# A layer norm without affine: one in-place ring of 48 rows a partition, tiles of 16 rows tapering to 8, 4, 2, 2

## Chip, cores, metric

One core of one Trainium2 chip. The metric is the device time of one execution in microseconds (us); several executions of each kernel were timed. A run also has a profile with the span from its first to its last instruction; the metric stands about 2 us above the span. "Fast" and "slow" are states of a run: one over 1.5% above the fastest of its kernel is called slow and left out of ratios.

## The reference

Every row of 1024 float32 numbers is brought to mean 0 and variance 1. There are 32 x 512 = 16384 rows, 67.1 MB in and 67.1 MB out.

```python
mean = np.mean(x, axis=-1, keepdims=True)
var = np.var(x, axis=-1, keepdims=True)
return ((x - mean) / np.sqrt(var + eps)).astype(np.float32)
```

## The kernel before

A tile takes 4 rows on each of 128 partitions (16 KiB of contiguous memory a partition, 2 MiB in all), so there are 32 tiles. Input and output have six buffers each. VectorE (DVE) makes the statistics, ScalarE (ACT) the square root and the normalisation, GpSimd (POOL) one small product. Loads are issued by SyncE (SP), stores by ACT.

```python
K = 4
...
xin = ctx.enter_context(tc.tile_pool(name="xin", bufs=6))
yout = ctx.enter_context(tc.tile_pool(name="yout", bufs=6))
...
for t in range(ntiles):
    xt = xin.tile([P, K, D], fdt)
    nc.sync.dma_start(out=xt, in_=x2[rows].rearrange("(p k) d -> p k d", p=P))
    # bn_stats on two halves of each row and bn_aggr: mv = mean, variance
    ...
    nc.vector.tensor_scalar_mul(out=negmean, in0=mv[:, :, 0], scalar1=-1.0)
    nc.vector.tensor_scalar(out=vpe, in0=mv[:, :, 1], scalar1=eps_val, ...)
    nc.vector.reciprocal(out=ivar, in_=vpe)
    nc.scalar.activation(out=rstd, in_=ivar, func=AF.Sqrt, ...)
    nc.gpsimd.tensor_mul(out=nmr, in0=negmean, in1=rstd)
    yt = yout.tile([P, K, D], fdt)
    for k in range(K):
        nc.scalar.activation(out=yt[:, k, :], in_=xt[:, k, :], func=AF.Identity,
                             bias=nmr[:, k : k + 1], scale=rstd[:, k : k + 1])
    nc.scalar.dma_start(out=dst, in_=yt)
```

The order of the source is not the order in which an engine issues its instructions. A scheduler lays that order down when the kernel is built.

## Time and profile before

| | |
|---|---|
| time | 321.08 us (320.97 to 321.26, 3 runs) |
| span of the profiled run | 319.0 us |
| busy | DVE 57%, ACT 48%, POOL 2% |
| rate while the stream is full | 431 GB/s |

The page's DMA row gives in tenths how busy the core's 16 DMA engines are in each of 40 slices of the span. An order-of-time line has start, duration, engine, source line, operation, output<-input, count, and in brackets the idle time before it with what ended it. A line of waits has the total in us, how often, and the longest.

### The profile page before, as it was taken

The numbers are of one execution on the slowest core, as the hardware profiler recorded it, in microseconds if no ns is written. First come the engines' busy times: TensorE is split into PE (matmuls) and PEld (weight loads), VectorE is DVE, ScalarE is ACT, GpSimd is POOL, SyncE is SP. The second block draws the span as 40 slices with busy tenths as digits, with TensorE's granted clock in tenths as the row PEclk, the third lists the DMA queues.
The fourth block names the chain that finished last, engine by engine and source line by source line (L and its number), as shares of the span: only waits on it lengthen the run. The fifth ranks groups of instructions, "written<-read, shape, count | busy, mean of one in ns | idle before, by whom it ended". The sixth has DMA issues, their size and how long they took to land.

```text
span 319.0 us, 926 instructions
## 1 busy us (share of the span) xinstructions
DVE 181.6 (57%) x480; ACT 154.3 (48%) x161; POOL 6.6 (2%) x36
## 2 busy tenths in 40 slices
DVE  0999764457754477544676355765446744467610
ACT  1147491651907419074380833809247091470970
POOL 0000000000000000000000000000000000000000
DMA  7999999999999999999999999999999999999995
GB/s 294 427 405 422 438 431 431 431 429 431 426 429 432 435 431 431 429 427 431 431 433 435 430 431 427 427 431 427 435 438 430 428 431 427 431 427 427 421 427 220
DMA packets 9222, 134.27 MB, mean 421 GB/s; under 512 B 1024, under 2 KB 1024, under 8 KB 1024
## 3 DMA queue, kind: packets, MB, share of 16 engines
q1 hardware_dynamic: 4608, 67.11, 49.6%
q10 hardware_dynamic: 4608, 67.11, 49.2%
q14 instruction: 6, 0.05, 0.0%
HBM read 67.11 MB, written 67.11 MB: 421 GB/s over the span
## 4 chain that ended last, share of the span: by engine, by line
DMA 87%; DVE 4%; issue 3%; ACT 2%; SPq 1%; POOLq 0%; POOL 0%; DVEq 0%
DMA xt<-in_x_dram 87%; DVE stats L53 3%; ACT yt L75 1%; SPq L47 1%; DVE mv L57 0%; DVE ivar L65 0%; DVE negmean L59 0%; POOLq L115 0%; ACT rstd L68 0%; POOL nmr L71 0%; DVE vpe L61 0%; DVEq L65 0%; DVEq L59 0%
## 5 line engine op out<-in xcount | busy, mean ns | idle before, releaser
L53 DVE BATCH_NORM_STATS2 stats<-xt 128x6 f32<-128x512 f32 x256 | 159.4, 665 | 115.3 <-DMA xt<-in_x_dram 115.3
L75 ACT ACTIVATE yt<-xt,nmr,rstd 128x1024 f32<-128x1024 f32 x128 | 146.7, 1227 | 4.7 <-POOL nmr L71 4.5
L68 ACT ACTIVATE rstd<-ivar 128x4 f32<-128x4 f32 x32 | 6.6, 205 | 149.6 <-DVE ivar L65 149.0
L57 DVE BATCH_NORM_AGGREGATE mv<-stats 128x2 f32<-128x12 f32 x128 | 25.1, 196 | 1.1
L71 POOL TENSOR_TENSOR nmr<-negmean,rstd 128x4 f32<-128x4 f32 x32 | 6.3, 198 | 297.9 <-ACT rstd L68 297.9
L65 DVE RECIPROCAL ivar<-vpe 128x4 f32<-128x4 f32 x32 | 5.7, 178 | 3.0
L59 DVE TENSOR_SCALAR negmean<-mv 128x4 f32<-128x4 f32 x32 | 5.4, 170 | 3.1
L61 DVE TENSOR_SCALAR vpe<-mv 128x4 f32<-128x4 f32 x32 | 5.2, 162 | 0.0
L68 ACT ACT_TABLE_LOAD x1 | 1.3, 1283 | 0.7 <-PEq L101 0.7
L101 POOL MEMSET const-float32-0.0<- 128x1 f32 x1 | 0.1, 98 | 0.2 <-issue 0.2
L101 POOL MEMSET const-uint8-127<- 128x1 uint8 x1 | 0.1, 102 | 0.0
L101 POOL MEMSET const-bfloat16-1.0<- 128x1 bf16 x1 | 0.1, 101 | 0.0
L101 POOL MEMSET const-float32-1.0<- 128x1 f32 x1 | 0.1, 98 | 0.0
## 6 DMA issues: line engine op xcount, KB each, us to landing
xt<-in_x_dram SPq DMA_DIRECT2D x32, 2048.0 KB, 38.4
out_dram<-yt ACTq DMA_DIRECT2D x32, 2048.0 KB, 15.5
```

What stands on the lines that cost most here:

```text
L47: nc.sync.dma_start(out=xt, in_=x2[rows].rearrange("(p k) d -> p k d", p=P))
L53: nc.vector.bn_stats(out=stats[:, k, s, :], in_=xt[:, k, s * BN_MAX : (s + 1) * BN_MAX],)
L57: nc.vector.bn_aggr(out=mv[:, k, :], in_=stats[:, k, :, :])
L59: nc.vector.tensor_scalar_mul(out=negmean, in0=mv[:, :, 0], scalar1=-1.0)
L61: nc.vector.tensor_scalar(out=vpe, in0=mv[:, :, 1], scalar1=eps_val, scalar2=None, op0=ALU.add)
L65: nc.vector.reciprocal(out=ivar, in_=vpe)
L68: nc.scalar.activation(out=rstd, in_=ivar, func=AF.Sqrt, bias=0.0, scale=1.0)
L71: nc.gpsimd.tensor_mul(out=nmr, in0=negmean, in1=rstd)
L75: nc.scalar.activation(out=yt[:, k, :], in_=xt[:, k, :], func=AF.Identity, bias=nmr[:, k : k + 1], scale=rstd[:, k : k + 1],)
L101: nc = _bacc.Bacc("TRN2", target_bir_lowering=False, num_devices=1)
```

## The change

The intent: fewer and larger DMAs with runs of 64 KiB (a DMA run is one contiguous piece of one partition, and one record in the DMA trace), no second set of buffers, and small last tiles so that the final store is short. The same 192 KiB of each partition now form one ring of 48 rows, in which a tile is loaded, normalised in place and stored. Statistics go by groups of 8 rows. The small operations are reordered: the square root is taken of the variance plus eps on ACT, then DVE takes the reciprocal and one fused product; POOL does nothing.

```diff
+TILES = (16, 16, 16, 16, 16, 16, 16, 8, 4, 2, 2)
+RING = 48
+GROUP = 8
...
-    xin = ctx.enter_context(tc.tile_pool(name="xin", bufs=6))
-    yout = ctx.enter_context(tc.tile_pool(name="yout", bufs=6))
+    ring = ring_pool.tile([P, RING, D], fdt)
...
+    for K in TILES:
+        if pos + K > RING:
+            pos = 0
+        xt = ring[:, pos : pos + K, :]
         nc.sync.dma_start(out=xt, in_=x2[rows].rearrange("(p k) d -> p k d", p=P))
+        for g in range(0, K, GROUP):
+            # bn_stats, bn_aggr for G rows
...
+            nc.scalar.activation(out=std[:, :G], in_=mv[:, :G, 1], func=AF.Sqrt, bias=eps_t, scale=1.0)
+            nc.vector.reciprocal(out=rstd[:, :G], in_=std[:, :G])
+            nc.vector.scalar_tensor_tensor(out=nmr[:, :G], in0=mv[:, :G, 0], scalar=-1.0,
+                                           in1=rstd[:, :G], op0=ALU.mult, op1=ALU.mult)
+            for k in range(G):
+                nc.scalar.activation(out=xt[:, g + k, :], in_=xt[:, g + k, :], func=AF.Identity, ...)
-        nc.scalar.dma_start(out=dst, in_=yt)
+        nc.scalar.dma_start(out=o2[rows].rearrange("(p k) d -> p k d", p=P), in_=xt)
```

More of the change, by code (lines that the diff above doesn't have):

```diff
@@ L26 @@
     BN_MAX = nc.vector.BN_STATS_FMAX
-    assert D % BN_MAX == 0
     NSUB = D // BN_MAX
-    K = 4
-    rows_per_tile = P * K
-    assert N % rows_per_tile == 0
-    ntiles = N // rows_per_tile
-    xin = ctx.enter_context(tc.tile_pool(name="xin", bufs=6))
-    yout = ctx.enter_context(tc.tile_pool(name="yout", bufs=6))
+    assert sum(TILES) * P == N
+    ring_pool = ctx.enter_context(tc.tile_pool(name="ring", bufs=1))
     st = ctx.enter_context(tc.tile_pool(name="st", bufs=4))
+    const = ctx.enter_context(tc.tile_pool(name="const", bufs=1))
     fdt = mybir.dt.float32
@@ L41 @@
     ALU = mybir.AluOpType
-    for t in range(ntiles):
-        rows = slice(t * rows_per_tile, (t + 1) * rows_per_tile)
-        xt = xin.tile([P, K, D], fdt)
-        nc.sync.dma_start(out=xt, in_=x2[rows].rearrange("(p k) d -> p k d", p=P))
-        stats = st.tile([P, K, NSUB, 6], fdt)
-        mv = st.tile([P, K, 2], fdt)
-        for k in range(K):
-            for s in range(NSUB):
-                nc.vector.bn_stats(
-                    out=stats[:, k, s, :],
-                    in_=xt[:, k, s * BN_MAX : (s + 1) * BN_MAX],
-                )
-            nc.vector.bn_aggr(out=mv[:, k, :], in_=stats[:, k, :, :])
-        negmean = st.tile([P, K], fdt)
-        nc.vector.tensor_scalar_mul(out=negmean, in0=mv[:, :, 0], scalar1=-1.0)
-        vpe = st.tile([P, K], fdt)
-        nc.vector.tensor_scalar(
-            out=vpe, in0=mv[:, :, 1], scalar1=eps_val, scalar2=None, op0=ALU.add
-        )
-        ivar = st.tile([P, K], fdt)
-        nc.vector.reciprocal(out=ivar, in_=vpe)
-        rstd = st.tile([P, K], fdt)
-        nc.scalar.activation(out=rstd, in_=ivar, func=AF.Sqrt, bias=0.0, scale=1.0)
-        nmr = st.tile([P, K], fdt)
-        nc.gpsimd.tensor_mul(out=nmr, in0=negmean, in1=rstd)
-        yt = yout.tile([P, K, D], fdt)
-        for k in range(K):
-            nc.scalar.activation(
-                out=yt[:, k, :],
-                in_=xt[:, k, :],
-                func=AF.Identity,
-                bias=nmr[:, k : k + 1],
-                scale=rstd[:, k : k + 1],
-            )
-        dst = o2[rows].rearrange("(p k) d -> p k d", p=P)
-        nc.scalar.dma_start(out=dst, in_=yt)
@@ new lines @@
+    ring = ring_pool.tile([P, RING, D], fdt)
+    eps_t = const.tile([P, 1], fdt)
+    nc.vector.memset(eps_t, eps_val)
+    row = 0
+    pos = 0
+    for K in TILES:
+        if pos + K > RING:
+            pos = 0
+        xt = ring[:, pos : pos + K, :]
+        rows = slice(row * P, (row + K) * P)
+        nc.sync.dma_start(out=xt, in_=x2[rows].rearrange("(p k) d -> p k d", p=P))
+        for g in range(0, K, GROUP):
+            G = min(GROUP, K - g)
+            stats = st.tile([P, GROUP, NSUB, 6], fdt, name="stats")
+            mv = st.tile([P, GROUP, 2], fdt, name="mv")
+            for k in range(G):
+                for s in range(NSUB):
+                    nc.vector.bn_stats(
+                        out=stats[:, k, s, :],
+                        in_=xt[:, g + k, s * BN_MAX : (s + 1) * BN_MAX],
+                    )
+                nc.vector.bn_aggr(out=mv[:, k, :], in_=stats[:, k, :, :])
+            std = st.tile([P, GROUP], fdt, name="std")
+            nc.scalar.activation(
+                out=std[:, :G], in_=mv[:, :G, 1], func=AF.Sqrt, bias=eps_t, scale=1.0
+            )
+            rstd = st.tile([P, GROUP], fdt, name="rstd")
+            nc.vector.reciprocal(out=rstd[:, :G], in_=std[:, :G])
+            nmr = st.tile([P, GROUP], fdt, name="nmr")
+            nc.vector.scalar_tensor_tensor(
+                out=nmr[:, :G],
+                in0=mv[:, :G, 0],
+                scalar=-1.0,
+                in1=rstd[:, :G],
+                op0=ALU.mult,
+                op1=ALU.mult,
+            )
+            for k in range(G):
+                nc.scalar.activation(
+                    out=xt[:, g + k, :],
+                    in_=xt[:, g + k, :],
+                    func=AF.Identity,
+                    bias=nmr[:, k : k + 1],
+                    scale=rstd[:, k : k + 1],
+                )
+        nc.scalar.dma_start(out=o2[rows].rearrange("(p k) d -> p k d", p=P), in_=xt)
+        row += K
+        pos += K
```

## The prediction

> **What bounds the kernel now.** I read the page first (parts 1, 2, 4 and 6), then the busy time by stretch, then the waits and the order of time on the engines.
>
> ```profile
> DVE 181.6 (57%) x480; ACT 154.3 (48%) x161; POOL 6.6 (2%) x36
> ...
> DMA  7999999999999999999999999999999999999995
> ...
> HBM read 67.11 MB, written 67.11 MB: 421 GB/s over the span
> ...
> DMA 87%; DVE 4%; issue 3%; ACT 2%; SPq 1%; POOLq 0%; POOL 0%; DVEq 0%
> ...
> out_dram<-yt ACTq DMA_DIRECT2D x32, 2048.0 KB, 15.5
> ```
>
> No compute engine is near full, and the DMA row is full from the second slice to the last but one. The busy time by stretch gives the rate of the full stream and its two ends:
>
> ```profile
> core 0: us, DVE busy (x) ACT busy (x) POOL busy (x), PEclk, DMA share, GB/s
> ...
> 60.00:200.00 140.00, 79.60 (x210) 69.26 (x73) 2.78 (x14) 1.00 1.01 431
> ...
> 314.00:316.00 2.00, 0.00 (x0) 0.00 (x0) 0.00 (x0) 1.00 0.66 279
> ...
> 317.00:318.00 1.00, 0.00 (x0) 0.00 (x0) 0.00 (x0) 1.00 0.04 16
> ```
>
> The stream runs at 431 GB/s. 134.27 MB at that rate take 311.5 us; the span is 319.0, so ramp and drain together cost only 7.5 us. A change here can win little unless the stream itself gets faster, but it can lose much if the stream runs dry. What could make it run dry shows in the order of time on ACT between 19 and 32 us:
>
> ```profile
> 19.61 0.38 ACTq L84 DMA_DIRECT2D out_dram<-yt  x1
> 20.11 0.21 ACT L68 ACTIVATE rstd<-ivar 128x4 f32<-128x4 f32 x1 [0.53 <-DVE ivar L65]
> 25.78 0.20 ACT L68 ACTIVATE rstd<-ivar 128x4 f32<-128x4 f32 x1 [5.47 <-DVE ivar L65]
> 25.89 5.75 ACT L75 ACTIVATE yt<-xt,nmr,rstd 128x1024 f32<-128x1024 f32 x5
> ```
>
> Tile 1's square root is done at 20.3, yet its four normalisations start only at 25.89: the scheduler has put tile 2's square root ahead of them, so ACT sits 5.47 us waiting for the statistics of a later tile. The list of waits says how common this is:
>
> ```profile
> ACT rstd L68 <- DVE ivar L65: 149.0, 19, 12.4
> ```
>
> With six input and six output buffers of 2 MiB this read-ahead costs nothing: the queues hold enough work while ACT waits.
>
> **What the Trainium skill says.**
> 1. DMA: Bandwidth & Descriptors, section "Where 436 GB/s comes from": a fabric ceiling of 435 GB/s. The trace agrees: 431. So larger runs can win at most about 1%, 311.5 to 308.7 us (estimate from that page's ceiling).
> 2. The same page, "Anatomy of one DMA": DMA engines do not wait on semaphores; the issuing sequencer does. So a load held back by a buffer, and a store held back by ACT, are absent from the queues. This kernel's trace agrees in the list of the DMA queue's own waits, where SP waits before it issues a load.
> 3. PSUM — Partial Sum Buffer, "Engine vs sequencer instructions": "ScalarE/VectorE/GpSimdE queues are strict FIFO." The 5.47 us above agree: work that was ready did not pass the square root ahead of it.
> 4. Perfetto Trace Analysis, "Optimization Strategy": consistent bubbles on the engine that should be saturated can mean too few buffers for the next tile. The DMA row before shows none; I expect the changed kernel to show them.
>
> **The change part by part.**
> Small work: 32 each of negmean (170 ns), vpe (162), reciprocal (178) go, 16.3 us of DVE; 18 groups with a reciprocal and one fused operation at about 180 ns come back, 6.5. DVE falls to about 172 us, ACT from 154.3 to about 151, POOL to nothing. All beside DMA: 0 us on the path.
> Descriptors: 64 KiB runs for 16 KiB and 22 DMAs for 64. Stream gain 0 to 3 us, see 1.
> Buffers: 12 x 16 KiB = 192 KiB a partition before, and 48 x 4 KiB = 192 KiB now; the bytes are equal but the grain is 3 slots of 8 MiB. Load k+3 waits for the whole store k. One big tile takes 8.39 MB / 431 = 19.5 us alone, 39 when a load and a store share.
> Order: I compared the instruction order of the two builds. In the new ACT stream the square root of tile 2's second group is followed by those of both groups of tile 3, and only then come tile 2's last eight normalisations. The same holds for tile 4 against both groups of tile 5. Store 2 therefore waits for load 3 and its statistics, store 4 for load 5. At the end, the square roots of the 8-, 4- and first 2-row tile precede the second half of tile 6; on DVE that half's reciprocal also follows the first statistics of the last tile. Also tile 6's first half comes behind three statistics instructions of the 8-row tile. So store 6, 8 MiB, waits until the very last load has landed: the taper is defeated.
>
> Worked timetable, from measured pieces: statistics 1.26 us a row (10.40 to 11.66 in the order of time, i.e. two halves and an aggregate), 20.2 a tile; normalisation 4.63/4 = 1.15 a row, 9.2 a group; 2.2 us per hand-off from a finished store to the next load's data (my choice: the first load is issued at 0.73 and used at 8.60, 3.0 us more than its 4.87 at 431, part of it ramp).
> - Loads 0, 1, 2 stream from 2. Load 0 lands at 22; group 0 is normalised at 36-45, group 1 at 46-55; store 0 is issued at 55, load 2 shares with it and lands at 65.
> - Store 0 ends at 80; load 3 needs it and nothing else is queued: idle 2.2.
> - Tile 1's second reciprocals sit behind tile 2's first statistics, so store 1 comes only at 93. Load 3 lands at 110, store 1 ends at 121.5: idle 2.2 again, load 4 from 124.
> - Statistics of tile 3 end at 130; tile 2's second half runs to 140; store 2 at 141. Load 4 lands at 145; store 3 at 159 and load 5 from 165 share to about 200.
> - Load 6 runs alone from 202 to 221.5. Store 4 waits for statistics of tile 5 (203-223), then ACT 224-233, issue 234, data 235.6: idle 14.
> - Store 4 alone to 255; then the last four loads (waiting for store 4) beside store 5. All that, 37 us of work, ends at 294.
> - The last load lands at 295; last statistics, then tile 6's second half 299-308; store 6 at 309.6, data 311: idle 16.6.
> - Stores 6 to 10 are 32 rows = 16.8 MB = 39 us: last byte at 350.
> Idle sum: 2.2 + 2.2 + 14.1 + 16.6 = 35. Span: 350 + 1.1 for the end (before: last packets in 317-318, span 319.0) = 351. The metric stood 2.1 above the span before (321.08 to 319.0): 353. Slow DMA engines: every idle is set by the slowest of 16, whose drift before was hidden by queued work; the drain from 314 to 318 shows some 2 us. For several exposed joints I add 2, and take 1 off for larger runs: **354 us**, +10%.
>
> **Rivals.**
> A. Stream stays full. If every tile were normalised when ready, a store would follow its landing by about 31 us (20.2 + 9.2 + small) within a 39 us period, and DMA would never idle: 308.7 to 311.5 plus 7.5, so 317 to 320 in span, 319 to 322 in the metric. For it: DVE 57%, ACT 48%. Against it: the order above is static, and 5.47 us show that ACT obeys it.
> B. Gain by larger runs plus the short last store: 314 to 318. Needs A and a faster stream; the ceiling leaves 1%, and the small last store can't help when store 6 waits for the last load.
> C. Unequal sharing. If the DMA engines alternate by descriptor, the 8-, 4- and 2-row loads (32, 16, 8 KiB runs) get a smaller share beside store 5 (64 KiB) and land later in the order; the same timetable with shares by size ends 8 us later: 362. Before, all runs are equal, so nothing in its trace speaks to it.
> D. Each hand-off costs 3.5 instead of 2.2: the timetable gives 8 us more, 362.
>
> **Range and chances.** The idle at 221 and 294 follow from static order and measured durations; errors are in rates and hand-offs. C and D push up, a faster stream at 435 pulls down by 3 to 4. Range 345 to 366. Slower by over 2% unless the order on the chip is not what the build shows: 0.93. Same 0.05 and faster 0.02 are A and B.
>
> **What would show it.** DMA row: two notches at about 80 and 122, and two real gaps of over 10 us at about 221-236 and 294-311. ACT's waits: square roots waiting for statistics with longest waits over 20 us. Store 6 issued after the last load has landed, five stores left in the last 40 us. DVE about 172, POOL about 0. Rate in full stretches 431 to 435. Wrong if the DMA row is full to the end (A), or if the gaps lie elsewhere: then the timetable's sharing is at fault; if the gaps are there but the last one is much longer, C.

## The result

The changed kernel took 361.31 us (360.94 to 361.8, 4 runs) against 321.12 for the kernel before in the same rounds: ratio 1.1253, 95% interval 1.1237 to 1.1269. A ratio here is the mean time of one kernel's fast runs over the mean of the other's fast runs of the same rounds, so it is not quite the ratio of the medians quoted. The results were correct.

The page of the changed kernel: busy time, the DMA row and the rate in each slice.

```profile
span 359.2 us, 663 instructions
...
DVE 166.7 (46%) x421; ACT 151.6 (42%) x147; POOL 0.2 (0%) x4
...
DMA  8998999988999599899998998089999890059998
...
GB/s 350 467 453 365 468 460 358 467 350 350 350 468 460 242 467 445 372 438 394 453 438 380 467 467 350 1 350 453 365 380 482 347 414 13 0 234 467 409 409 350
```

Every engine has become less busy, and the stream that was full from end to end now has two holes. (The rate row books a run of 64 KiB in the slice in which it starts, so single slices swing.) The busy time by stretch gives the holes; the columns are DVE, ACT and POOL busy with counts, clock, DMA share, GB/s:

```profile
225.00:237.00 12.00, 11.86 (x33) 10.54 (x11) 0.00 (x0) 1.00 0.21 88
297.00:319.00 22.00, 12.17 (x37) 14.28 (x17) 0.00 (x0) 1.00 0.11 49
```

The records of single DMA runs give their edges: nothing in flight at 81.5-82.9, 124.1-125.8, 225.1-236.8 and 297.5-318.7 us, in sum 36.0. Three of the four longest rows in the changed kernel's list of waits:

```profile
ACT std L69 <- DVE mv L67: 123.9, 10, 36.4
ACT ring L84 <- DVE nmr L75: 60.4, 8, 36.6
DVE rstd L73 <- ACT std L69: 32.5, 3, 24.7
```

Before, the longest wait of ACT for statistics was 12.4 us; now two waits of over 36 us stand there. What they held up shows on ACT in order of time:

```profile
180.18 0.28 ACT L69 ACTIVATE std<-mv,eps_t 128x8 f32<-128x8 f32 x1
216.86 0.30 ACT L69 ACTIVATE std<-mv,eps_t 128x8 f32<-128x8 f32 x1 [36.39 <-DVE mv L67]
226.46 0.30 ACT L69 ACTIVATE std<-mv,eps_t 128x8 f32<-128x8 f32 x1 [9.30 <-DVE mv L67]
226.72 10.29 ACT L84 ACTIVATE ring<-ring,nmr,rstd 128x1024 f32<-128x1024 f32 x9
235.91 0.34 ACTq L92 DMA_DIRECT2D out_dram<-ring  x1
...
290.80 9.16 ACT L84 ACTIVATE ring<-ring,nmr,rstd 128x1024 f32<-128x1024 f32 x8 [36.62 <-DVE nmr L75]
...
306.66 0.30 ACT L69 ACTIVATE std<-mv,eps_t 128x2 f32<-128x2 f32 x1 [2.28 <-DVE mv L67]
308.65 10.29 ACT L84 ACTIVATE ring<-ring,nmr,rstd 128x1024 f32<-128x1024 f32 x9 [1.70 <-DVE nmr L75]
317.84 0.34 ACTq L92 DMA_DIRECT2D out_dram<-ring  x1
```

At 180 us the square root for tile 4's second half is done. The two square roots that follow belong to tile 5 and wait until 226; only then come the eight normalisations of tile 4 (the ninth is already tile 5's) and, at 235.9, store 4. At the end the same happens to tile 6, whose store waits for the square root of a 2-row tile at 306.7. DVE holds both tiles too:

```profile
206.03 1.88 DVE L63 BATCH_NORM_STATS2 stats<-ring 128x6 f32<-128x512 f32 x3 [34.95 <-DMA ring<-in_x_dram]
...
226.34 0.22 DVE L73 RECIPROCAL rstd<-std 128x8 f32<-128x8 f32 x2
...
288.09 1.88 DVE L63 BATCH_NORM_STATS2 stats<-ring 128x6 f32<-128x512 f32 x3 [40.59 <-DMA ring<-in_x_dram]
289.88 0.18 DVE L73 RECIPROCAL rstd<-std 128x8 f32<-128x8 f32 x1
...
308.23 0.26 DVE L73 RECIPROCAL rstd<-std 128x8 f32<-128x8 f32 x2
```

The reciprocal of tile 4's second half, whose square root was done at 180.5, is one of the two at 226.34: it stands behind all statistics of tile 5, which began at 206.03. So ACT's order and DVE's each hold store 4 until tile 5 has landed. Tile 6's first half did not start before 290.8 because its reciprocal, at 289.88, is queued behind statistics of the 8-row tile, whose load only landed at 288; the second half's, at 308.23, is queued behind the first statistics of the last tile.

### The profile page after: what moved, and what is told of

Read it like the earlier page. It is cut to its first block, busy times and chain, and to the rows that moved or that the text cites. A ratio compares the mean times of both kernels' runs of the same rounds, so it can differ in the third digit from the quotient of the medians.

```text
span 359.2 us, 663 instructions
## 1 busy us (share of the span) xinstructions
DVE 166.7 (46%) x421; ACT 151.6 (42%) x147; POOL 0.2 (0%) x4
## 2 busy tenths in 40 slices
DMA packets 3172, 134.25 MB, mean 374 GB/s; under 512 B 352, under 2 KB 352, under 8 KB 352
## 4 chain that ended last, share of the span: by engine, by line
DMA 54%; DVE 21%; ACT 17%; issue 2%; SPq 0%; ACTq 0%
DMA ring<-in_x_dram 34%; DMA out_dram<-ring 20%; DVE stats L63 19%; ACT ring L84 16%; DVE mv L67 2%; ACT std L69 0%; DVE rstd L73 0%; DVE nmr L75 0%; SPq L55 0%; ACTq L84 0%; ACTq L92 0%
## 5 line engine op out<-in xcount | busy, mean ns | idle before, releaser
L63 DVE BATCH_NORM_STATS2 stats<-ring 128x6 f32<-128x512 f32 x256 | 158.2, 659 | 133.6 <-DMA ring<-in_x_dram 133.6
L84 ACT ACTIVATE ring<-ring,nmr,rstd 128x1024 f32<-128x1024 f32 x128 | 145.9, 1227 | 60.4 <-DVE nmr L75 60.4
L69 ACT ACTIVATE std<-mv,eps_t 128x8 f32<-128x8 f32 (+2 forms) x18 | 5.2, 293 | 123.9 <-DVE mv L67 123.9
L73 DVE RECIPROCAL rstd<-std 128x8 f32<-128x8 f32 (+2 forms) x18 | 2.8, 172 | 32.7 <-ACT std L69 32.5
L75 DVE SCALAR_TENSOR_TENSOR nmr<-mv,rstd 128x8 f32<-128x8 f32 (+2 forms) x18 | 2.7, 151 | 0.1
```

The lines of the kernel that those rows point to most:

```text
L63: nc.vector.bn_stats(out=stats[:, k, s, :], in_=xt[:, g + k, s * BN_MAX : (s + 1) * BN_MAX],)
L69: nc.scalar.activation(out=std[:, :G], in_=mv[:, :G, 1], func=AF.Sqrt, bias=eps_t, scale=1.0)
L73: nc.vector.reciprocal(out=rstd[:, :G], in_=std[:, :G])
L75: nc.vector.scalar_tensor_tensor(out=nmr[:, :G], in0=mv[:, :G, 0], scalar=-1.0, in1=rstd[:, :G], op0=ALU.mult, op1=ALU.mult,)
L84: nc.scalar.activation(out=xt[:, g + k, :], in_=xt[:, g + k, :], func=AF.Identity, bias=nmr[:, k : k + 1], scale=rstd[:, k : k + 1],)
```

## The experiments

Theory O: the order of issue ties a store to a later tile's load; with three slots of 8 MiB that starves both DMA queues. Rival G: the coarse ring does it by itself, whatever the order. Rival L: working in place, or runs of 64 KiB, is slow on the DMA engines. Eleven kernels ran, all with correct results. None of them removes a wait for data; edges of issue order add no semaphore.

### 1. Pin the order

Each instruction of ACT and DVE gets an edge to the one that the source writes before it on the same engine.

```diff
+    def order(made):   # issue order alone, no semaphore
+        ins = made.ins
+        before = last.get(ins.engine)
+        if before is not None:
+            tc.add_manual_dep(ins, before, mybir.DependencyInfo(
+                mybir.DependencyClass.NoSync, mybir.DependencyReason.DATA), reason="program order")
+        last[ins.engine] = ins.name
+        return made
...
-            nc.scalar.activation(out=std[:, :G], ...)
+            order(nc.scalar.activation(out=std[:, :G], ...))   # likewise each ACT and DVE instruction of the loop
```

> The changed kernel, with edges of issue order alone that pin ACT's and DVE's instructions to the order in which the source writes them; tiles, ring, bytes and waits for data as in the changed kernel. Theory O (the order of issue starves the queues): both long gaps of the DMA row (225-237 and 297-319 us) and the two notches go, 318 us, range 316 to 322, that is 0.99 to 1.00 of the kernel before. Rival G (a grain of three 8 MiB slots is too coarse in itself): the gaps between a finished store and the next load stay, over 335 us. Rival L (in place, or 64 KiB runs, are slow on the DMA engines): rate in full stretches under 420 GB/s and no gain, near 361.

Measured: fast runs 322.35 to 323.53 us, ratio 1.0052 (1.0035 to 1.0069) to the kernel before. The DMA row has no hole:

```profile
DVE 181.8 (57%) x421; ACT 153.4 (48%) x147; POOL 0.2 (0%) x4
...
DMA  9999999899999999999999999998999999999997
```

Order alone is worth 361.3 - 322.9 = 38 us of the 40 lost. Rival G falls: the same three slots stay full. Rival L falls as a main cause. The time missed my range by a microsecond or so, and three of six runs took 331 to 332 us; they count as slow and have no profile, so what they show stays open. Even against them the order would be worth 30 us.

### 2. Pin only the end

The edges are made from tile 6 on (`if before is not None and row >= 96`).

> The changed kernel with the order pinned only from tile 6 on (its last 16-row tile and the taper); tiles 0 to 5 keep the scheduler's order. Theory O says the two long gaps are separate: the gap at 297-319 goes or shrinks under 5 us, the one at 225-237 and the notches stay. 338 us, range 333 to 343. If the last gap came from loads landing late beside the store (unequal shares of the DMA engines) and not from order: it stays at over 10 us, over 350.

Measured: 342.46 us, ratio 1.0664. The records of DMA runs show holes at 81.6-83.0, 124.3-126.1 and 228.6-237.9 us (one run in flight from 226.4), and none after that but a dip of half a microsecond at 327. So the last hole has its own cause in the order of the end, and it cost 361.3 - 342.5 = 19 us; the holes that stayed go when the rest is pinned as well (experiment 1).

### 3. Pin ACT alone

> The changed kernel with only ACT pinned to source order; DVE is left to the scheduler, which still puts tile n's reciprocals behind statistics of tile n+1. Theory O in its narrow form (ACT's square roots that read ahead are the whole cause): the gaps go, 322 to 331 us as with both pinned. Theory O in its wide form (any reciprocal or square root that stands behind a later tile's statistics ties a store to a later load): pinning ACT alone only spreads the gaps, several of 2 to 4 us and one of over 12 before the last stores, 358 us, range 348 to 364.

```diff
+        if ins.engine != mybir.EngineType.Activation:
+            return made
```

Measured: 358.72 us, ratio 1.1167. Holes at 81, 124, 146, 169, 211, 234, 255 (1.3 to 2.7 us each) and 297.3-317.4. The narrow form of O is wrong: with ACT in source order, DVE still holds reciprocals behind a later tile's statistics, and that alone keeps most of the loss. The list of waits shows ACT's normalisations waiting for DVE's product:

```profile
ACT ring L104 <- DVE nmr L95: 149.3, 18, 32.6
```

DVE pinned alone was not run.

### 4. Fine grain in the same ring, in the scheduler's order

`TILES = (4,) * 32`, `GROUP = 4`: twelve slots of 2 MiB, in place, no edges.

> The changed kernel with 32 tiles of 4 rows and groups of 4 in the same ring in place (12 slots of 2 MiB instead of 3 of 8 MiB), and the scheduler's own order, which still issues the next tile's square root ahead of each store. Theory O in its full form (order hurts because a read-ahead of one tile is a third of the ring): read-ahead of 1/12 of the ring costs nothing, DMA row full, 320 us, range 317 to 323. If in-place itself were the loss (a load must wait for a store where before it waited for ACT alone): over 330.

Measured: 325.71 us, ratio 1.0139 (1.0126 to 1.0152): a miss. I had looked at ACT's order alone. On DVE the scheduler had put each reciprocal behind the statistics of tiles up to seven places on. ACT then runs that far behind the loads, and when they are done its backlog sets the pace:

```profile
275.38 4.63 ACT L84 ACTIVATE ring<-ring,nmr,rstd 128x1024 f32<-128x1024 f32 x4 [4.89 <-DVE nmr L75]
279.92 0.28 ACT L69 ACTIVATE std<-mv,eps_t 128x4 f32<-128x4 f32 x1
280.05 0.34 ACTq L92 DMA_DIRECT2D out_dram<-ring  x1
280.64 4.63 ACT L84 ACTIVATE ring<-ring,nmr,rstd 128x1024 f32<-128x1024 f32 x4 [0.44 <-DVE nmr L75]
```

From 275 to 317 us one 2 MiB tile comes every 5.26 us, where the stream could take one in 4.87 (2.097 MB at 431 GB/s): that is 399 GB/s.

### 5. The same with the order pinned

> The fine-grain kernel (32 tiles of 4 rows, 12 slots, in place) with the order pinned as well. Its first version ran at 325.7 us: ACT fell seven tiles behind the loads, because the reciprocals stand behind the statistics of later tiles, and the last stores came at ACT's pace of 5.26 us a tile (275 to 317 us) with the DMA row at 390 GB/s. Theory O: with pinned order ACT stays within a tile of the loads, the tail goes, 320.5 us, range 318.5 to 322. If in-place costs by itself: stays at 324 or more.

Measured: 320.89 us, ratio 0.9992 (0.9979 to 1.0004). At this grain working in place costs nothing that shows, and neither does the new small work; the grain of before plus the order of the source is as good as the kernel before.

### 6. The kernel before, with ACT pinned

Edges on its square roots, normalisations and stores.

> The kernel before, ACT pinned to source order in the same way. Theory O says its six input and six output buffers already hide the read-ahead: same time within 0.5 percent (319.5 to 322.5), though the list of waits loses most of ACT's 149 us behind later tiles' statistics. If order mattered at any grain: faster by over 1 percent.

Measured: 321.75 us, ratio 1.0013 (1.0001 to 1.0025). As expected in time: twelve buffers of 2 MiB hide the read-ahead. The other half of the expectation was wrong: ACT's wait for statistics stays 143.1 us. It now waits for its own tile instead of the next one, and ACT, busy for half of the span, waits as long as before.

### 7. No taper, in both orders

`TILES = (16,) * 8`, first in the scheduler's order, then pinned.

> The changed kernel without the taper (eight tiles of 16 rows), scheduler's order. The timetable that gave the changed kernel: store 6 waits for load 7 and both its groups' statistics, gap from about 293 to 326, then two whole tiles are stored: 370 us, range 364 to 376. The taper then saved about 9 us even under the bad order. If the taper's unequal runs had been what hurts (small loads starved beside a large store), removing it would help: under 358.

> Pinned order without the taper (eight tiles of 16 rows). Load 7 lands with only store 6 left beside it; 20 us of statistics and 19 of normalisation of one tile lie before its last store: timetable gives one gap of about 16 us near 294-311 and nothing else: 335 us, range 331 to 341, that is 12 more than with the taper. If the taper did nothing: 323.

Measured: 371.55 us (ratio 1.1568, last hole 298.3-329.4) and 338.25 us (ratio 1.0526 over its fast runs, last hole 301.2-315.5; one run of four took 347.8, slow). The taper does what it was meant for: it saves 371.6 - 361.3 = 10 us in the bad order and 338.3 - 322.9 = 15 in the good one. So the taper is no part of the loss.

### 8. Unequal runs in and out

A store after each group: 64 KiB runs in, 32 KiB out; then groups of 4 rows, 16 KiB out. Order pinned.

```diff
-        order(nc.scalar.dma_start(out=o2[rows].rearrange(...), in_=xt))
+            order(nc.scalar.dma_start(out=o2[rows].rearrange(...)[:, g : g + G, :], in_=xt[:, g : g + G, :]))
```

> Pinned order, 16-row loads, but a store after each group of 8 rows (32 KiB runs out, 64 KiB runs in). Theory C (the DMA engines alternate between the two queues by run, so bytes are shared as run sizes): beside a full store queue the 8-row load of the taper had 131 against 301 GB/s in the pinned kernel; here runs of 32 KiB stand on both sides and it gets half, and in mixed stretches of 16-row loads the loads get two parts in three. Time 320, range 317 to 323, as stores start 9 us earlier. If shares were by queue, not by run: half and half in every mixed stretch.

> As the one before, with groups and stores of 4 rows (16 KiB runs out, 64 KiB in). Theory C: where both queues hold work, loads get four parts in five (345 against 86 GB/s); stores lag, loads then wait for free slots, but the queues are never both empty: 321, range 318 to 326. If shares were by queue: half and half.

Measured: 319.45 us (ratio 0.9952, 0.9938 to 0.9965) and 323.45 us (1.0071, 1.0039 to 1.0102). Spreading each record's bytes over its duration gives the rates in stretches in which both queues hold work:

```
kernel, stretch (us)                     loads   stores  GB/s
64 KiB in, 32 KiB out,  56 to 64          303      131
64 KiB in, 16 KiB out,  48 to 56          344       88
pinned, 32 KiB in, 64 KiB out, 252-264    131      301
```

The share goes by run size, 2:1, 4:1 and 1:2, not half and half. The same shows in the DMA view of the changed kernel between 258 and 282 us, where tile 5's store (64 KiB runs) and the load of the 8-row tile (32 KiB) meet; q10 carries stores, q1 loads, and the numbers are runs, MB, share of the engines (the load's first run starts only at 261.8, so its part is below a third):

```profile
q10 hardware_dynamic: 112, 7.34, 75.7%
q1 hardware_dynamic: 92, 3.01, 29.4%
```

### 9. Tiles of 8 rows

`TILES = (8,) * 15 + (4, 2, 2)`, order pinned: six slots of 4 MiB.

> Pinned order, in place, tiles of 8 rows (32 KiB runs, 6 slots), tapering 4, 2, 2. Hypothesis T (turns): in the pinned kernel with 16-row tiles the loads running when a store stream sets in beside them are stretched, 5 us in all over five places, because few large tiles make the two queues run dry in turn; 6 slots keep both queues filled, one turn only, as in the kernel before. With 606 ns per 16 KiB (measured for 32 KiB runs) against 611: 317.5 us, range 316 to 320. If turns were not the cause and run size mattered more: no better than 322.

Measured: 318.67 us (318.65 to 319.71), ratio 0.9932 (0.992 to 0.9945). It has the lowest median of all, not clear of experiment 8's first kernel (319.45, with overlapping intervals), and beats the kernel before by 0.7%. The records of the DMA runs agree with hypothesis T:

```
                         duration for 16 KiB, ns    stretched beyond that, us
                         (median of a load run)     (over 16 engines, whole run)
before, 16 KiB runs               611                        1.8
tiles of 8, 32 KiB                606.5                      1.6
pinned, 64 KiB                    604.5                      5.5
changed kernel, 64 KiB            604.5                      7.8
```

Larger runs make the stream faster by 0.7% (434 against 431 GB/s), but something is given back where a stream starts. In the changed kernel about 3.2 of the 7.8 us lie in loads that are in flight when a store stream sets in (at 56, 95 and 143 us, up to 4072 ns for 64 KiB instead of 2418), about 2.3 in the first runs of a load stream, with no store setting in beside them (at 1.7, 82.9, 125.8 and 205), and 1.5 in store runs, most of them when load 7 sets in at 258. The pinned kernel, whose two queues run dry in turn, has several such turns; 8-row tiles have one, at 36 us, besides the start. How long the runs are stretched is measured, and the 3.9 us less of it fit the 4 us gained; why they are stretched is not settled.

## Why the prediction was right

354 us was predicted, 345 to 366 as the range, and 361.31 measured. Of the rivals, A (a full stream) and B are out and the main line held, with C on top of it. D (3.5 us for each hand-off) did not come true at the notches, where 1.4 and 1.7 us were idle. The timetable against the trace:

| step | predicted, us | measured, us |
|---|---|---|
| store 0 issued | 55 | 55.1 |
| store 1 issued | 93 | 93.5 |
| store 2 issued | 141 | 142.4 |
| store 3 issued | 159 | 161.3 |
| store 4 issued | 234 | 235.9 |
| store 6 issued | 309.6 | 317.8 |
| last byte | 350 | 357.9 |
| idle at the two notches | 2.2, 2.2 | 1.4, 1.7 |
| idle at the two holes | 14.1, 16.6 | 11.7, 21.2 |

- *Bound.* DMA it was and is. For 36 us of the changed kernel no DMA run is in flight; before, there was no such stretch.
- *Small work.* ACT 151.6 and POOL 0.2 as said; DVE 166.7, not 172. The same 421 instructions in source order are busy for 181.8 us (experiment 1), so a sum of durations does not give DVE's busy time here; why is open. It lies beside the stream either way.
- *Order.* The step on which the prediction rests, that the two builds' static order decides, is shown by experiments 1, 2 and 3. Experiment 3 adds that ACT's part cannot be mended alone: that won back only 361.3 - 358.7 = 2.6 us. The prediction named DVE's reciprocals for tiles 1 and 6; for store 4 it named ACT alone, and DVE held that one as well.
- *Idle sum.* 35 predicted, 36.0 measured. Its parts were less exact, and that they cancel is luck: the notches were 1.3 us shorter together, the first hole 2.4 shorter (load 6 landed at 225.1, not 221.5) and the last 4.6 longer. The latter fits rival C, a share by run size, which I had kept out of the sum: load 7 got 29% of the engines beside store 5, not half, and landed at 288. Part of that is a late start and not the share: it was issued at 256.8 and its first run began at 261.8, 5.0 us where the timetable allowed 2.2. (A store issued on idle engines began after 0.8 us, at 236.8 and 318.7; store 0, issued beside a running load, after 4.6.) DVE then had 16 rows of statistics, 20 us, to do before 308, so in this order tile 6's second half could not start earlier. No run tests equal shares in this order, so C's part in the 4.6 us is read from the trace.
- *The term that was too small* is the rest beside full stream and idle. The timetable left 350 - 311.5 - 35.1 = 3.4 us for it, and "for several exposed joints I add 2" made it 5.4. Measured over 434 GB/s, the changed kernel loses 48.6 us of DMA time up to its last byte at 357.9: 36.0 idle and 12.6 of this rest, of which 7.8 are stretched runs (1.8 before), 1.7 lie ahead of the first byte and 3.1 are what is left, put down to engines that start or stop unevenly. The 7.2 us too few here account for the distance from 354 to 361, since the idle time (0.9 more) and the faster stream (2.2 gained, 1 allowed for) nearly cancel.
- *Larger runs* gave 134.25 MB / 431 - 134.25 / 434 = 2.2 us, within the 0 to 3 named.
- *Taper.* "The taper is defeated" was too strong: experiment 7 shows 10 us of benefit even so.

## What to carry to other kernels

When a kernel is bound by DMA, look at what may keep the next transfer out of the queue before looking at the transfers: here the same bytes in the same ring took 361 or 323 us by nothing but the order in which two half-idle engines issue their work. Read the built order of each engine whenever tile sizes change, on every engine in the chain: an instruction that stands behind a later tile's work ties this tile's store to that tile's load, which cost nothing with six input and six output buffers (experiment 6), 4.8 us with twelve slots in place, where DVE read seven tiles ahead (325.7 against 320.9), and 38 us with three. Choose the grain from both sides: larger runs won 0.7% of rate, and 8-row tiles in six slots kept it where 16-row tiles gave it back.

## What the Trainium skill lacked or had wrong

- DMA: Bandwidth & Descriptors, "Queues, rings and completion order", tells that an engine alternates between queues packet by packet. It does not say what follows for two queues whose runs differ: here bytes went 303:131 for 64 against 32 KiB, and 344:88 for 64 against 16.
- SBUF — State Buffer, "The DMA setup-cost knee", advises the largest single transfer one can make. It has no word on the grain against the ring: with the order pinned, 8 MiB transfers in three slots took 322.9 us, 4 MiB in six 318.7, 2 MiB in twelve 320.9.
- Perfetto Trace Analysis, "Optimization Strategy", gives too few buffers as what repeated bubbles can mean. Here the bubbles (36.0 us idle) went away with the same buffers and another order, 361.3 to 322.9 us.
- No page tells that runs are stretched where a stream sets in, beside another or after a standstill: up to 4072 ns against 2418 for a load run of 64 KiB, 7.8 us over the changed kernel.
- No page gives a measured gain of long runs above 16 KiB: 611 ns for 16 KiB in runs of that size, 606.5 in runs of 32 KiB, 604.5 in runs of 64 KiB.
